# Attention in a two-layer trunk: merge weights applied three heads later through DRAM, output product begun between the last heads' steps

## The chip, the core and the metric

The kernel runs on one core of a Trainium2 chip. The core has five engines with a queue each: TensorE (PE, matmuls and transposes), VectorE (DVE), ScalarE (ACT), GpSimd (POOL) and SyncE (SP); here SP issues every DMA. The metric is device time in microseconds (us) of one launch. The profile is of one execution and names times from the first instruction of its span.

## The reference, cut to what matters

Layer 1 of the trunk mixes tokens by dilated attention: 12 heads in 3 groups of 4 (dilations 1, 4, 16). A group's output is weighted by a softmax over the three groups of a head index, and the 12 weighted outputs go through one output product.

```python
def dilated_attention_mixer(u, w_qkv, w_out, cos, sin):
    ...
    for gi, (window, dilation) in enumerate(DILATED_GROUPS):
        o_g, lse_g = dilated_window_group(q[:, :, hs], k[:, :, hs], v[:, :, hs], window, dilation)
    ...
    alpha = jax.nn.softmax(lse, axis=2)
    o = (o * alpha[..., None]).reshape(B, S, ATTN_WIDTH).astype(u.dtype)
    return o @ w_out
```

All is float32, SEQ = 1024, D_MODEL = 1024, head size 128. After the mixer come the residual, a norm and a dense feed-forward (FFN), then the final norm.

## The kernel before

Activations lie with 128 features on the partitions and 1024 tokens along the row, so a tile is 128x1024 float32. Products are made of pairs: each operand is split into a rounded part and a rest (a cast on ACT, a subtraction on DVE), and three matmuls of 512 columns stand for one (`split`, line 139, `mm3`, line 118, `seeded`, line 706).

The attention pass goes through 12 heads in the order `heads` (line 923): j = 0 to 3 and, within a j, the groups gi = 0, 1, 2. For each head `attn_qk` (line 779) loads two weight tiles, makes seven operands of them (a to g, `pair_weights`, line 691) and runs seven products of 12 matmuls (`pair`, line 727), with rotary embedding (`rope`, line 765) on what comes out. After each product stands a `tick()` (line 720): it runs the steps that `later` put down for this count. So the steps of one head are written between the products of the next: before the change scores at +1 (`s1`) and +3 (`s2`, which ends with the softmax `soft`), the merge weights of a j at +3 after its third head (`attn_weights`, line 892), the transposes of the probabilities at +6 and +8 (`t1`, `t2`), and the product with the values at +10 (`values`, line 874), whose result goes to the DRAM tensor `od`. Seven ticks make one head.

After the last head the remaining ticks run with no product between them (line 938). Then, for all 12 heads, line 943 loads the output from `od`, line 945 loads its merge weight broadcast to all partitions, line 946 multiplies, and line 947 splits the result. `mixer_out` (line 574) then makes eight output tiles in the order `DORDER` (0, 4, 1, 5, ...), each from the 12 splits: 72 matmuls of 512 columns per output tile (12 heads, two halves, three passes).

Tiles come from pools with a fixed number of slots: `ws` 4 (probabilities `ap`, and now the merge tiles), `wx` 2, `vc` 8 (q, k, values, outputs, the two rotary tables), `va` 16 and `vb` 12 (the pass's operands, later the splits), PSUM `mm` 4 and `ax` 4. A request waits for a slot of its tag to come free. The framework's planner fixes the order of each engine's queue from the program's order and its own estimate of when things are ready, so an instruction can stand ahead of its place in the program; the queue is then worked off in that order.

Of the kernel before, what the change touches and what calls it, by code (L numbers as in the profile page):

```python
# [15 lines left out]
P = 128  # L16
T = 1024
# [3 lines left out]
NH = 12  # L21
# [19 lines left out]
def trunk_kernel(ctx, tc, x, cols, consts, w_in, w_hout, w_qkv, w_aout, w_ffn, w_down, out):  # L41
    nc = tc.nc
# [8 lines left out]
    def big(tag, name, dt=F32):  # L51
        return gp.tile([P, T], dt, tag=tag, name=name, bufs=slots[tag])
# [4 lines left out]
    def mmps(name):  # L57
        return pmm.tile([P, 512], F32, tag="mm", name=name)
# [4 lines left out]
    def hs(hh):  # L63
        return slice(hh * 512, hh * 512 + 512)
# [13 lines left out]
    for k in range(KT):  # L78
        t = big("vc", f"x{k}")
# [32 lines left out]
    def load_w(src, n, name, tag="wr"):  # L112
        raw = early.pop(name, None)
        if raw is None:
            raw = load_raw(src, n, name, tag)
        return split_w(raw[:, 0:n], n, name, (256,) if name == "f0" else ())
# [93 lines left out]
    nm = Norm("n0")  # L210
# [7 lines left out]
    for i0 in range(0, NMASK, 8):  # L218
        n = min(8, NMASK - i0)
# [351 lines left out]
        ["vb"] * 2 + ["ws"] * 3 + ["va"] * 16 + ["vb"] * 7,  # L571
    )

    def mixer_out(l, spill, load, vs, parts, name):
        nrm = Norm(name)
        h, ops = {}, {}

        def weights(d):
            n = len(vs) // parts * P
            return [load_w((w_hout, w_aout)[l][d][:, i * n:i * n + n], n, f"{name}w{d}_{i}") for i in range(parts)]  # L580

        for d in DORDER:
            t = big("vc", f"{name}h{d}")
            nc.sync.dma_start(t[:], load[d])
            ws = weights(d)
            if d == KT - 1:
                w_head[l] = ffn_w_head(l, 0)
            ps = [mmps(f"p_{name}{d}_{hh}") for hh in range(2)]
            m = len(vs) // parts
            for i, (whi, wlo) in enumerate(ws):  # L590
                mm3(ps, whi, wlo, 0, vs[i * m:i * m + m], first=(i == 0), last=(i == parts - 1))
            h[d] = add_res(ps, t, d, nrm, spill, 2 * l + 1, name)
            if d >= 4:
                ops[d - 4] = ffn_operands(d - 4, h[d - 4], h[d], op_tags[l][7 * (d - 4):7 * (d - 3)], name)
        return ops, nrm
# [4 lines left out]
    nm = Norm("n2")  # L600
# [116 lines left out]
    def later(n, step):  # L717
        steps.setdefault(n, []).append(step)

    def tick():  # L720
        for step in steps.pop(clock[0], ()):
            step()
        clock[0] += 1
# [55 lines left out]
    def attn_qk(j, gi):  # L779
        n = gi * 4 + j  # L780
        ga = load_raw(w_qkv[n], D, f"aq{n}")
        up = load_raw(w_qkv[NH + n], D, f"ak{n}")
        sz = big("wx", f"sz{n}")
        s5, z = sz[:, 0:512], sz[:, 512:T]
        p = pair(ga, up, qops, s5, f"a{n}")
        q = big("vc", f"aq{n}")
        k = big("vc", f"ak{n}")
        rope(q, next(p), None, 0, z)
        rope(k, next(p), s5, 1, z)
        rope(q, next(p), s5, 1, z)  # L790
        rope(k, next(p), None, 0, z)
        for _ in p:
            pass
        return q, k
# [49 lines left out]
    def attn_value(j, gi):  # L844
        n = gi * 4 + j
        vv = big("vc", f"avv{n}")
        src = vd[:, cs(n)]
        if gi == 0:
            nc.sync.dma_start(vv.rearrange("p (c m) -> p c m", m=P), src.rearrange("(c p) m -> p c m", p=P))
        elif gi == 1:  # L850
            sv = src.rearrange("(i p r) m -> p r i m", p=P, r=4)
            for r in range(4):
                nc.sync.dma_start(vv[:, r * 256:r * 256 + 256].rearrange("p (i m) -> p i m", m=P), sv[:, r])
        else:
            nc.sync.dma_start(vv.rearrange("p (c m) -> p c m", m=P), src.rearrange("(p c) m -> p c m", c=8))
        return vv

    od = dp.tile([NH, P, T], F32, name="od")

    def attn_out(j, gi, blocks, ptiles):  # L860
        dil = (1, 4, 8)[gi]
        n = gi * 4 + j
        pts = {}
        groups = [(t, g1, where[g1:g1 + 4]) for t, where in ptiles for g1 in range(0, len(where), 4)]

        def turn(gs):
            for t, g1, grp in gs:
                ps = axps(f"apx{n}_{grp[0][0]}_{grp[0][1]}")
                for c, key in enumerate(grp):
                    pts[key] = t[:, cs(g1 + c)]  # L870
                    nc.tensor.transpose(ps[:, cs(c)], pts[key], ident)
                nc.scalar.copy(t[:, g1 * P:(g1 + len(grp)) * P], ps[:, 0:len(grp) * P])

        def values(vv):
            o = big("vc", f"ao{n}")
            for hh in range(2):
                ps = axps(f"apo{n}{hh}")
                for b in range(4 * hh, 4 * hh + 4):
                    ks = blocks[b][1]
                    for i, kc in enumerate(ks):  # L880
                        nc.tensor.matmul(ps[:, cs(b % 4)], vv[:, cs(kc)], pts[(b, kc)], start=(i == 0), stop=(i == len(ks) - 1))
                if dil == 1:
                    nc.scalar.copy(o[:, hs(hh)], ps[:])
                else:
                    r = dil // 2
                    sl = slice(hh * r, hh * r + r)
                    nc.scalar.copy(o.rearrange("p (i r) -> p r i", r=dil)[:, sl, :], ps.rearrange("p (r i) -> p r i", r=r))
            nc.sync.dma_start(od[n], o[:])

        return (lambda: turn(groups[:2])), (lambda: turn(groups[2:])), values  # L890

# [29 lines left out]
        return dw  # L921

    heads = [(j, gi) for j in range(4) for gi in range(3)]
    dws = {}
    sts = [sp.tile([P, 3, 8, 2], F32, tag="st", name=f"st{j}", bufs=2) for j in range(4)]
    for i, (j, gi) in enumerate(heads):
        q, k = attn_qk(j, gi)
        blocks, ptiles, s1, s2 = attn_scores(j, gi, sts[j], q, k)
        t1, t2, values = attn_out(j, gi, blocks, ptiles)
        at = clock[0]  # L930
        later(at + 1, s1)
        later(at + 3, s2)
        if gi == 2:
            later(at + 3, lambda j=j: dws.setdefault(j, attn_weights(j, sts[j])))
        later(at + 6, t1)
        later(at + 8, t2)
        later(at + 10, lambda j=j, gi=gi, values=values: values(attn_value(j, gi)))
    while steps:
        tick()
    ov = []  # L940
    for i, (j, gi) in enumerate(heads):
        o = big("vc", f"am{j}_{gi}")
        nc.sync.dma_start(o[:], od[gi * 4 + j])
        wb = big("wx", f"wb{j}_{gi}")
        nc.sync.dma_start(wb[:], dws[j][gi].partition_broadcast(P))
        nc.vector.tensor_mul(o[:], o[:], wb[:])
        ov.append(split(o, "va" if i < 8 else "vb", f"aov{i}"))

    ops, nm = mixer_out(1, hd[2], hd[1], ov, 2, "n3")
    act1 = dp.tile([NF, P, T], F32, name="act1")  # L950
    ffn_in(1, ops, nm, act1)

# [112 lines left out]
```

## Time and profile before

| what | us |
|---|---|
| median of 3 runs | 2611.85 |
| lowest, highest | 2607.98, 2612.05 |
| the profiled execution | 2608.14 |
| its span, first to last instruction | 2606.3 |
| PE busy in the span | 2536.5 |

The attention pass takes about 1412 to 1754 us of the span; from there to about 1825 lie the last heads' steps, the merges, and the first two output tiles. The page gives busy time by engine and the chain of work that ended last; the trace answers for a stretch, an engine, a line or a tile.

### The profile page before, as it was taken

The numbers are of one execution on the slowest core, as the hardware profiler recorded it, in microseconds if no ns is written. First come the engines' busy times: TensorE is split into PE (matmuls) and PEld (weight loads), VectorE is DVE, ScalarE is ACT, GpSimd is POOL, SyncE is SP. The second block draws the span as 40 slices with busy tenths as digits, with TensorE's granted clock in tenths as the row PEclk, the third lists the DMA queues.
The fourth block names the chain that finished last, engine by engine and source line by source line (L and its number), as shares of the span: only waits on it lengthen the run. The fifth ranks groups of instructions, "written<-read, shape, count | busy, mean of one in ns | idle before, by whom it ended". The sixth has DMA issues, their size and how long they took to land.

```text
span 2606.3 us, 30492 instructions
## 1 busy us (share of the span) xinstructions
PE 2536.5 (97%) x11804; PEld 2103.7 (81%) x11804; DVE 1741.4 (67%) x3070; ACT 909.5 (35%) x1400; POOL 129.9 (5%) x107
## 2 busy tenths in 40 slices
PE   8999999999999999999999999998999999999998
PEld 6888888788888888888888777776878888888887
DVE  7888888977877777433613666655477777775336
ACT  5222222344323233212523555653343323332212
POOL 1111111111000000000000000000010000000000
PEclk9999999999999999999999999997999999999999
DMA  4111111142222224531232222227422222236323
GB/s 144 33 33 33 33 33 33 43 144 89 76 87 81 89 81 147 181 104 61 97 105 75 74 66 66 74 90 253 135 81 89 81 89 81 81 102 229 110 58 127
DMA packets 108144, 240.48 MB, mean 92 GB/s; under 512 B 23008, under 2 KB 50016, under 8 KB 108000
## 3 DMA queue, kind: packets, MB, share of 16 engines
q1 hardware_dynamic: 108000, 238.54, 27.9%
q8 instruction: 93, 1.52, 0.2%
q14 instruction: 51, 0.42, 0.1%
HBM read 185.93 MB, written 52.58 MB: 92 GB/s over the span
## 4 chain that ended last, share of the span: by engine, by line
PE 79%; DVE 10%; ACT 4%; DMA 4%; issue 2%; POOL 1%; SPq 0%; POOLq 0%; DVEq 0%; ACTq 0%
PE pt L482 6%; PE pt L483 6%; PE pt L481 6%; PE pfw L125 6%; PE pfw L127 6%; PE pfw L124 6%; PE pb L482 4%; PE pb L483 4%; PE pb L481 4%; PE p_n L125 2%; PE p_n L127 2%; PE p_n L124 2%; PE pv L654 2%; PE pv L655 2%; PE pv L656 2%
## 5 line engine op out<-in xcount | busy, mean ns | idle before, releaser
L563 DVE TENSOR_TENSOR h<-pfw,h 128x512 f32<-128x512 f32 (+1 forms) x104 | 63.6, 645 | 197.6 <-PE pfw L127 197.5
L108 ACT CAST h_fw<-r_fw 128x896 fp32r<-128x896 f32 (+1 forms) x60 | 58.3, 973 | 237.7 <-PE pfw L125 219.5
L108 ACT CAST h_fa<-r_fg 128x1024 fp32r<-128x1024 f32 x44 | 46.5, 1056 | 198.3 <-PE pt L482 183.5
L108 ACT CAST h_fb<-s 128x1024 fp32r<-128x1024 f32 x44 | 46.4, 1054 | 171.1 <-PE pb L482 159.6
L829 PE MATMUL as<-ak,aq 128*128 128x256 f32 (+1 forms) x192 | 65.4, 459 | 20.2 <-DVE ak L777 17.0
L342 DVE COPY_PREDICATED at<-lm,lv 128x192 f32<-128x192 uint8 (+2 forms) x288 | 82.1, 353 | 4.0 <-PE lv L327 3.2
L156 POOL TENSOR_TENSOR rs_n<-ms_n,half 128x8 f32<-128x8 f32 (+2 forms) x7 | 9.3, 1335 | 1357.7 <-DVE ms_n L154 1357.7
L655 PE MATMUL pv<-vw,qb 128*128 128x512 f32 x192 | 74.8, 390 | 0.0
L654 PE MATMUL pv<-vw,qb 128*128 128x512 f32 x192 | 74.8, 389 | 0.0
L656 PE MATMUL pv<-vw,qb 128*128 128x512 f32 x192 | 74.7, 389 | 0.0
L494 DVE TENSOR_TENSOR s<-r_fu 128x512 f32<-128x512 f32 x44 | 30.3, 691 | 64.0 <-DMA r_fu<-in_w_ffn_dram 63.9
L829 PEld LDWEIGHTS as<-ak,aq 128*128 128x128 f32 x192 | 46.0, 279 | 33.6 <-issue 9.2
L482 PE MATMUL pb<-n3b,h_fa 128*128 128x512 f32 x176 | 68.7, 390 | 2.6 <-DVE n3b L456 2.6
L109 DVE TENSOR_TENSOR l_fw<-r_fw,h_fw 128x896 fp32r<-128x896 f32 (+1 forms) x60 | 67.1, 1121 | 4.9 <-ACT h_fw L108 4.3
L482 PE MATMUL pb<-n1b,h_fa 128*128 128x512 f32 x176 | 68.6, 390 | 1.2 <-DVE n1b L456 1.2
L481 PE MATMUL pb<-n3b,h_fa 128*128 128x512 f32 x176 | 68.8, 391 | 0.7 <-ACT n3b L455 0.6
L481 PE MATMUL pb<-n1b,h_fa 128*128 128x512 f32 x176 | 68.6, 390 | 0.0
L481 PE MATMUL pt<-n1t,h_fb 128*128 128x512 f32 x176 | 68.6, 390 | 0.0
L481 PE MATMUL pt<-n3t,h_fb 128*128 128x512 f32 x176 | 68.6, 389 | 0.0
L483 PE MATMUL pb<-n3b,l_fa 128*128 128x512 f32 x176 | 68.5, 389 | 0.0
L483 PE MATMUL pb<-n1b,l_fa 128*128 128x512 f32 x176 | 68.5, 389 | 0.0
L482 PE MATMUL pt<-n3t,h_fb 128*128 128x512 f32 x176 | 68.5, 389 | 0.0
(1504 smaller groups left out, 7939.8 us busy)
## 6 DMA issues: line engine op xcount, KB each, us to landing
r_fu<-in_w_ffn_dram SPq DMA_DIRECT2D x44, 512.0 KB, 3.6
r_fg<-in_w_ffn_dram SPq DMA_DIRECT2D x44, 512.0 KB, 3.6
act<-g SPq DMA_DIRECT2D x44, 512.0 KB, 2.6
st<-act SPq DMA_DIRECT2D x44, 512.0 KB, 4.3
r_fw<-in_w_down_dram SPq DMA_DIRECT2D x44, 448.0 KB, 3.4
h<-hd SPq DMA_DIRECT2D x16, 512.0 KB, 6.3
r_fw<-in_w_down_dram SPq DMA_DIRECT2D x16, 512.0 KB, 3.7
vr<-in_w_qkv_dram SPq DMA_DIRECT2D x24, 256.0 KB, 3.3
```

The lines of the kernel that those rows point to most:

```text
L108: nc.scalar.copy(hi[:, a:b], src[:, a:b])
L124: nc.tensor.matmul(p[:, 0:b - a], wh, vh[:, a:b], start=(first and i == 0), stop=False)
L125: nc.tensor.matmul(p[:, 0:b - a], wh, vl[:, a:b], start=False, stop=False)
L127: nc.tensor.matmul(p[:, 0:b - a], wl, vh[:, a:b], start=False, stop=(last and i == n - 1))
L342: nc.vector.copy_predicated(av[:, :, d:4, :], mk[:, :, d:4, :], pv[:, :, s0:s0 + 4 - d, :])
L481: nc.tensor.matmul(ps[:], wh, bh, start=(kk == 0), stop=False)
L482: nc.tensor.matmul(ps[:], wh, bl, start=False, stop=False)
L483: nc.tensor.matmul(ps[:], wl, bh, start=False, stop=(kk == 3))
L654: nc.tensor.matmul(ps[:], vh, wh, start=(kb == 0), stop=False)
L655: nc.tensor.matmul(ps[:], vh, wl, start=False, stop=False)
L656: nc.tensor.matmul(ps[:], vl, wh, start=False, stop=(kb == 7))
L829: nc.tensor.matmul(ps[:, o:o + w], tok(q, gi, b * P, P), tok(k, gi, ks[0] * P, w), start=True, stop=True)
```

## The change

- The steps of a head move later: scores from +1 and +3 to +2 and +4, transposes from +6 and +8 to +9 and +11, the values product from +10 to +13. The load of the values (`attn_value`) moves from the values step to the first transposes.
- `attn_merge(j - 1)`, after the products of the third head of j: for each of three heads and two halves, load half an output (256 KB) and the broadcast weights (256 KB) into one `ws` tile, multiply on DVE, store back to `od`. Eighteen round trips in all, for j = 0, 1, 2.
- The three outputs of j = 3 stay in SBUF (`late`), and are multiplied there.
- After the loop the nine merged outputs are loaded and split without a multiply. The first two output tiles are begun in between the last steps of the last head: heads 0 to 5 of each, then 6 to 8, and at the end 9 to 11 (`part_out`). `mixer_out` takes them over through `begun`.

```diff
--- before.py
+++ after.py
@@ -571,7 +571,7 @@
         ["vb"] * 2 + ["ws"] * 3 + ["va"] * 16 + ["vb"] * 7,
     )
 
-    def mixer_out(l, spill, load, vs, parts, name):
+    def mixer_out(l, spill, load, vs, parts, name, begun={}):
         nrm = Norm(name)
         h, ops = {}, {}
 
@@ -582,10 +582,10 @@
         for d in DORDER:
             t = big("vc", f"{name}h{d}")
             nc.sync.dma_start(t[:], load[d])
-            ws = weights(d)
+            ws = () if d in begun else weights(d)
             if d == KT - 1:
                 w_head[l] = ffn_w_head(l, 0)
-            ps = [mmps(f"p_{name}{d}_{hh}") for hh in range(2)]
+            ps = begun.get(d) or [mmps(f"p_{name}{d}_{hh}") for hh in range(2)]
             m = len(vs) // parts
             for i, (whi, wlo) in enumerate(ws):
                 mm3(ps, whi, wlo, 0, vs[i * m:i * m + m], first=(i == 0), last=(i == parts - 1))
@@ -857,6 +857,8 @@
 
     od = dp.tile([NH, P, T], F32, name="od")
 
+    late = []
+
     def attn_out(j, gi, blocks, ptiles):
         dil = (1, 4, 8)[gi]
         n = gi * 4 + j
@@ -885,7 +887,10 @@
                     r = dil // 2
                     sl = slice(hh * r, hh * r + r)
                     nc.scalar.copy(o.rearrange("p (i r) -> p r i", r=dil)[:, sl, :], ps.rearrange("p (r i) -> p r i", r=r))
-            nc.sync.dma_start(od[n], o[:])
+            if j < 3:
+                nc.sync.dma_start(od[n], o[:])
+            else:
+                late.append(o)
 
         return (lambda: turn(groups[:2])), (lambda: turn(groups[2:])), values
 
@@ -921,32 +926,67 @@
         return dw
 
     heads = [(j, gi) for j in range(4) for gi in range(3)]
+    def attn_merge(j):
+        for gi in range(3):
+            o = od[gi * 4 + j]
+            for hh in range(2):
+                t = big("ws", f"mg{j}_{gi}_{hh}")
+                oh, wb = t[:, 0:512], t[:, 512:T]
+                nc.sync.dma_start(oh, o[:, hs(hh)])
+                nc.sync.dma_start(wb, dws[j][gi][hs(hh)].partition_broadcast(P))
+                nc.vector.tensor_mul(oh, oh, wb)
+                nc.sync.dma_start(o[:, hs(hh)], oh)
+
     dws = {}
     sts = [sp.tile([P, 3, 8, 2], F32, tag="st", name=f"st{j}", bufs=2) for j in range(4)]
     for i, (j, gi) in enumerate(heads):
         q, k = attn_qk(j, gi)
+        if gi == 2 and j:
+            attn_merge(j - 1)
         blocks, ptiles, s1, s2 = attn_scores(j, gi, sts[j], q, k)
         t1, t2, values = attn_out(j, gi, blocks, ptiles)
+        vv = {}
         at = clock[0]
-        later(at + 1, s1)
-        later(at + 3, s2)
+        later(at + 2, s1)
+        later(at + 4, s2)
         if gi == 2:
-            later(at + 3, lambda j=j: dws.setdefault(j, attn_weights(j, sts[j])))
-        later(at + 6, t1)
-        later(at + 8, t2)
-        later(at + 10, lambda j=j, gi=gi, values=values: values(attn_value(j, gi)))
-    while steps:
-        tick()
-    ov = []
-    for i, (j, gi) in enumerate(heads):
+            later(at + 4, lambda j=j: dws.setdefault(j, attn_weights(j, sts[j])))
+        later(at + 9, lambda t1=t1, vv=vv, j=j, gi=gi: (vv.setdefault(0, attn_value(j, gi)), t1()))
+        later(at + 11, t2)
+        later(at + 13, lambda values=values, vv=vv: values(vv[0]))
+
+
+    ov, begun, aw = [], {}, {}
+    for i, (j, gi) in enumerate(heads[:9]):
         o = big("vc", f"am{j}_{gi}")
         nc.sync.dma_start(o[:], od[gi * 4 + j])
-        wb = big("wx", f"wb{j}_{gi}")
-        nc.sync.dma_start(wb[:], dws[j][gi].partition_broadcast(P))
+        ov.append(split(o, "va" if i < 8 else "vb", f"aov{i}"))
+
+    def part_out(d, lo, hi):
+        if d not in begun:
+            begun[d] = [mmps(f"p_n3{d}_{hh}") for hh in range(2)]
+        i = lo // 6
+        if (d, i) not in aw:
+            aw[d, i] = load_w(w_aout[d][:, i * 768:i * 768 + 768], 768, f"n3w{d}_{i}")
+        mm3(begun[d], *aw[d, i], (lo - 6 * i) * P, ov[lo:hi], first=(lo == 0), last=(hi == NH))
+
+    d0, d1 = DORDER[:2]
+    at = clock[0]
+    for upto, d, lo, hi in ((2, d0, 0, 6), (4, d1, 0, 6), (9, d0, 6, 9), (11, d1, 6, 9), (13, None, 0, 0)):
+        while clock[0] <= at + upto:
+            tick()
+        if d is not None:
+            part_out(d, lo, hi)
+    for gi in range(3):
+        o = late[gi]
+        wb = big("wx", f"wb{gi}")
+        nc.sync.dma_start(wb[:], dws[3][gi].partition_broadcast(P))
         nc.vector.tensor_mul(o[:], o[:], wb[:])
-        ov.append(split(o, "va" if i < 8 else "vb", f"aov{i}"))
-
-    ops, nm = mixer_out(1, hd[2], hd[1], ov, 2, "n3")
+        ov.append(split(o, "vb", f"aov{9 + gi}"))
+    for d in (d0, d1):
+        part_out(d, 9, NH)
+
+    ops, nm = mixer_out(1, hd[2], hd[1], ov, 2, "n3", begun)
     act1 = dp.tile([NF, P, T], F32, name="act1")
     ffn_in(1, ops, nm, act1)
```

## Rows read from the trace of the kernel before

**Rows 1.** The page, parts 1 and 2: engine, busy us; granted clock in 40 slices.

```profile
PE 2536.5 (97%) x11804; PEld 2103.7 (81%) x11804; DVE 1741.4 (67%) x3070; ACT 909.5 (35%) x1400; POOL 129.9 (5%) x107
...
PEclk9999999999999999999999999997999999999999
```

**Rows 2.** Windows: stretch, length, busy us (instructions) by engine, clock, DMA share, GB/s.

```profile
1616.00:1705.00 89.00, 83.94 (x405) 68.95 (x405) 56.38 (x135) 52.20 (x118) 0.00 (x0) 1.00 0.24 71
1735.00:1754.40 19.40, 19.40 (x97) 16.14 (x95) 9.10 (x24) 6.96 (x11) 0.00 (x0) 1.00 0.41 123
1754.40:1761.40 7.00, 3.21 (x14) 1.39 (x13) 3.87 (x7) 6.89 (x22) 0.00 (x0) 0.82 0.07 1
1761.40:1770.00 8.60, 8.22 (x40) 8.02 (x40) 3.38 (x18) 1.75 (x5) 0.00 (x0) 0.75 0.54 170
1770.00:1778.00 8.00, 6.72 (x24) 4.75 (x24) 0.00 (x0) 5.81 (x20) 0.00 (x0) 0.66 0.29 77
1778.00:1783.50 5.50, 0.03 (x1) 0.03 (x1) 1.73 (x5) 2.10 (x3) 0.00 (x0) 0.50 0.74 239
1783.50:1793.00 9.50, 8.58 (x19) 5.80 (x20) 6.51 (x10) 2.13 (x3) 0.00 (x0) 0.50 0.87 289
1793.00:1815.30 22.30, 20.27 (x85) 15.35 (x84) 17.76 (x17) 8.82 (x9) 0.00 (x0) 1.00 0.90 318
1815.30:1825.10 9.80, 9.80 (x43) 7.72 (x42) 6.36 (x7) 3.15 (x4) 0.00 (x0) 1.00 0.85 334
1825.10:1909.00 83.90, 83.90 (x371) 69.32 (x370) 33.97 (x45) 25.17 (x35) 5.16 (x4) 1.00 0.38 124
```

**Rows 3.** Waits of PE over the attention pass, 1412 to 1754: total, times, longest.

```profile
PE as L829 <- DVE ak L777: 14.1, 8, 2.6
PE as L829 <- DVE st L830: 3.1, 3, 1.3
PE p_a L710 <- DVE ak L768: 0.6, 1, 0.6
```

**Rows 4.** Chain that ended last, 1768 to 1783 us: start, us, what.

```profile
1773.58 5.52 DMA dn<-st
...
1780.15 6.01 DMA am<-od
```

**Rows 5.** Timeline of VectorE, a 512-column multiply, the tail's multiply and split.

```profile
1636.88 0.69 DVE L774 TENSOR_TENSOR sz<-sz,sb 128x512 f32<-128x512 f32 x1 [3.51 <-ACT sz L771]
...
1781.11 1.23 DVE L946 TENSOR_TENSOR am<-am,wb 128x1024 f32<-128x1024 f32 x1 [11.62 <-DMA am<-od]
...
1783.45 1.23 DVE L145 TENSOR_TENSOR aov0l<-am,aov0h 128x1024 fp32r<-128x1024 f32 x1 [0.59 <-ACT aov0h L144]
```

**Rows 6.** DMA issues: tensors, count, KB each, us from issue to landing (page; pass).

```profile
vr<-in_w_qkv_dram SPq DMA_DIRECT2D x24, 256.0 KB, 3.3
...
od<-ao SPq DMA_DIRECT2D x12, 512.0 KB, 2.6
...
wb<-dw SPq DMA_DIRECT2D x2, 512.0 KB, 4.6
```

**Rows 7.** Timeline of the SP queue, third cycle of the pass.

```profile
1639.53 0.34 SPq L72 DMA_DIRECT2D r_aq<-in_w_qkv_dram  x1
...
1690.28 0.33 SPq L902 DMA_DIRECT2D cm<-dn  x1
...
1696.24 0.37 SPq L920 DMA_DIRECT2D dw<-ae  x1
```

**Rows 8.** Timeline of ScalarE: a cast that waited for its load, a tail split.

```profile
1676.37 0.62 ACT L611 CAST a7a<-r_aq 128x512 fp32r<-128x512 f32 x1 [3.02 <-DMA r_aq<-in_w_qkv_dram]
...
1782.37 1.04 ACT L144 CAST aov0h<-am 128x1024 fp32r<-128x1024 f32 x1 [3.40 <-DVE am L946]
```

**Rows 9.** Timeline of PE, one scores row and the first product of a head.

```profile
1642.88 2.16 PE L829 MATMUL as<-ak,aq 128*128 128x256 f32 x4 [1.47 <-DVE ak L777]
...
1664.84 0.39 PE L710 MATMUL p_a<-qb,a3a 128*128 128x512 f32 x1
```

## The prediction, made blind

> **What bounds the kernel now.** I read the page first: PE is busy for 2536.5 of 2606.3 us [rows 1], so a gain has to come from stretches in which PE idles or runs slowly. The clock line has one dip, in slice 28, where attention ends and the output product begins. Then the windows, cut at the places where PE's work changes [rows 2]. In a cycle of three heads (1616 to 1705) PE is busy 83.94 of 89.0 us; from 1735 to 1754.4, where the last products run, all of the time. Then it falls: 3.21 of 7.0, 8.22 of 8.6, 6.72 of 8.0, 0.03 of 5.5 us. From 1783.5 to 1793 the granted clock is 0.50, which of the two levels is 1.2 GHz, after PE did almost nothing from 1778 on, and 19 matmuls take 9.5 us. From 1793 the clock is full, but 22.3 us hold 85 matmuls with the DMA engines at 0.90. Only from 1815.3 does the output product run dense.
>
> The waits of PE in the pass itself come next [rows 3]: 14.1 us in 8 waits for the rotated k, the longest 2.6, and 3.1 for the maxima of the scores. Last the chain [rows 4]: the end of the softmax at 1773.58, a 5.52 us store of its sums, then a 6.01 us load of an output just stored. These are round trips through DRAM with nothing beside them.
>
> **The tail, in numbers.** Dense, a matmul of 512 columns costs 83.9 / 371 = 0.226 us [rows 2]. The two first output tiles are 144 of them, 32.6 us. The last heads' transposes, scores and values products are the 3.21 + 8.22 + 6.72 = 18.2 us of PE from 1754.4 to 1778 [rows 2]. Together 50.8 us of work stand in 70.7 us (1754.4 to 1825.1): 19.9 us are lost, and that is the most this end can give.
>
> **What the change makes of the tail.** It removes the serial merge: nine multiplies of 1.23 us on DVE [rows 5], nine broadcast loads [rows 6] and the wait for the last store before the first load; 108 of the 144 matmuls (24.4 us) may run before the last merge weights exist. They go where PE now idles. What still ends last is the chain of the last j. From the end of its softmax: 5.52 us to store the sums [rows 4]; 5.96 us from their load to the store of the weights, as in the cycle before, where no merge stood in DVE's way [rows 7]; that store's landing, for which I take the 2.6 of a store of outputs [rows 6]; 4.6 for the broadcast load [rows 6]; 1.23 to multiply [rows 5] and 1.04 to cast [rows 8]. That is 21 us to the first matmul of head 9. DVE then spends 1.23 + 1.23 us per head on multiply and rest [rows 5], so head 11 is split some 26 us after the softmax and the two tiles are done at 28. If the softmax ended at 1773.6 as now, that is 1801.6, and PE's own sum, 1754.4 + 50.8 = 1805.2, would end last.
>
> It won't end that early, since **slots** are added to the wait. The six merge tiles of j = 2 are requested before the probability tile of the last head, and both come from the four `ws` slots. Two slots come free with the values of head 9, which now run three ticks later, about at the last product (1754); the other two with the values of head 10, well after that. I take it that slots go in order of request. One round of two merge tiles costs a 256 KB load, 3.3 us [rows 6], two multiplies of 512 columns, 1.4 [rows 5], and a store, at most like the 2.6 of one twice its size [rows 6]: 7.3 us, three rounds 22. So the last head's scores have a place at about 1776, the softmax ends near 1785 (now 1773.6), and 28 us later is 1813. Against 1825.1 this gives 12 us; the ends are 19.9 (slots free at once) and 4 (each round loads in the 6.01 us of the load in [rows 4], 2.7 longer, so all is 8 us later). I stay at 12, since the 256 KB row is the nearest in size. A gap of PE before the last three heads is in this forecast; what it may do to the clock is a rival below.
>
> The loads of heads 0 to 8 ask for `vc` slots: the tables, q and k of head 11 and one kept output hold five, so three are open at first, enough for one round of loads and splits in 7 us while the products end. The splits cost 9 x 1.23 us on DVE [rows 5], which had 9.10 + 3.87 + 3.38 + 0 + 1.73 = 18.1 us of work in the 48.5 from 1735 to 1783.5 [rows 2]. They are covered there; without that cover they would cost the 11 us.
>
> **What it makes of the pass.** Scores one tick later put one more product, 12 x 0.226 = 2.7 us, between rope and scores. Every wait for k is at most 2.6 us [rows 3], as the 1.47 before one [rows 9], so the 14.1 us can go in full; at the other end nothing, if the planner puts the scores where it does now. Transposes and values moved later only lengthen lives: q and k are given back one tick later, and the next head's tiles ask a head later. I cost this at nothing, covered by the seven ticks of the next head; without it, the wait for k would come back. I take 11 of the 14.1, as some waits will move to the 3.1 us kind.
>
> The merges of j = 0 and 1 lie inside the pass. DVE gets 12 multiplies of 0.69 us, 8.3 us, in cycles in which it is busy 56.4 of 89 [rows 2]: hidden. SP gets 36 more issues a third of a microsecond each; the queue is idle most of the time, and the next head's weights are ordered at 1639.53 [rows 7] for a product that starts at 1664.84 [rows 9], some 20 us early. What isn't hidden by itself is **waiting in order**: a store waits for its multiply and holds SP's later loads; a multiply waits for two loads and holds DVE's rope and splits, on which PE waits a product later. The trace has no such wait in the pass. Its bounds: a gain is excluded, since nothing is removed there; the low end is nothing, if loads land when the planner expects them; the high end a wait like the 3.02 us of a cast for its load [rows 8] in each of three rounds, 9 us a merge, 18 for two. I take 1.5 us a merge, 3 in all, near the low end, because the weights' loads with 20 us in hand show that DVE's next piece is seldom due at once. So the pass gives 11 - 3 = 8 us.
>
> **Sum.** 12 + 8 = 20 us. The profiled execution, 2608.14 (span 2606.3 and 1.84 around it), becomes 2588; it lay 3.7 us under the median of the runs, so the forecast for the median is 2611.85 - 20 = 2592.
>
> **The rivals.**
> - Slots are no hindrance and the waits vanish whole: 19.9 + 14.1 = 34, 2578. For it: 50.8 us of PE work with no other bound. Against: the order of requests. Chance 0.12.
> - The half clock comes back. PE has 24.4 + 18.2 = 42.6 us to do before the last three heads and is done at 1797, the first matmul of head 9 comes at 1806: 9 us of idling, longer than the 5.5 in which the clock stands at 0.50 now [rows 2]. The last 36 matmuls (8.2 us) and what follows would run at half rate as the 19 do, which took 9.5 us for 4.3 of work: 5 us more, 2597. Chance 0.12. The Trainium skill ("TensorE: Matmul & The Clock Gate", HAM oscillation) says that a gap in which PE idles brings the throttle back and the next group starts cold; the trace agrees, 0.50 from 1778 on.
> - The planner puts the scores where they stood: no 11 us, 12 - 3 = 9, 2603. Chance 0.08.
> - The merges eat the gain: 18 us of waits against 11 + 12, 2607. Within 0.2% of no change. Chance 0.10.
> - **Slower**: DVE stands still behind a multiply or a maximum that waits for a slot, for most of a merge. Three rounds are 22 us; PE can go on for two products, 5.4, before its PSUM tiles are full, so up to 17 us stop per merge, 51 for three, against 25 gained by tail and waits: 2611.85 + 26 = 2638. It decides from 25 / 3 = 8 us a merge on. For it: DVE and SP work in order, and `ws` is shared with the probabilities. Against: the values of the third head before free two slots within a head. Chance 0.13.
>
> The forecast itself has 0.45, its own range 2583 to 2601.
>
> **How the numbers follow.** 0.2% (5.2 us) is about what a measurement of this kernel can tell from no change. Faster: 0.45 + 0.12 + 0.12 + 0.08 = 0.77. Same 0.10, slower 0.13. The range takes in the best case and the one in which the merges eat the gain, and leaves out the slower one: 2577 to 2612.
>
> **What would show it.** In the profile after: fewer and shorter waits of PE for k (14.1 to under 4); matmuls of the output product between 1754 and 1778; clock full there; `dn` stored later than 1773.6; the third output tile begun near 1813 less the 8 of the pass. Wrong would be: VectorE rows that wait for the merge's loads or for its slot for more than a few us, PE rows in the cycle after a merge waiting for DVE, or weights' loads on SP behind a store of `od`.

## The result, and the profile after

| | before | after |
|---|---|---|
| median, us (4 runs each) | 2611.02 | 2633.68 |
| span of the profiled execution | 2606.3 | 2630.1 |
| start of the last matmul of the pass's last product | 1754.17 | 1772.12 |
| start of the first matmul of the third output tile | 1825.11 | 1846.56 |

After over before is 1.0088, 95% interval 1.007 to 1.0105: slower by 22.7 us, where 20 us less were forecast. By the two marks in the table 17.9 us were lost in the attention pass and 3.5 in the tail (from the pass's end to the third output tile: 70.9 us before, 74.4 after).

First the page of after, part 1: busy time by engine.

```profile
PE 2538.7 (97%) x11804; PEld 2110.8 (80%) x11804; DVE 1739.6 (66%) x3079; ACT 908.0 (35%) x1400; POOL 129.9 (5%) x107
```

Over the whole span PE does the same 11804 matmuls in nearly the busy time of [rows 1] (2538.7 against 2536.5 us); what grew is idle time. The windows of after say where (columns as in [rows 2]).

```profile
1437.00:1526.50 89.50, 83.82 (x394) 69.04 (x392) 56.48 (x135) 52.03 (x118) 0.00 (x0) 0.98 0.22 67
1526.50:1616.00 89.50, 78.75 (x365) 65.70 (x366) 52.22 (x122) 42.87 (x94) 0.00 (x0) 0.92 0.35 102
1616.00:1705.00 89.00, 80.15 (x370) 65.06 (x368) 50.55 (x112) 46.07 (x108) 0.00 (x0) 0.96 0.41 114
...
1778.00:1786.00 8.00, 2.95 (x10) 2.47 (x11) 3.57 (x5) 2.98 (x5) 0.00 (x0) 0.59 0.91 291
...
1819.00:1836.00 17.00, 6.77 (x50) 6.10 (x48) 4.04 (x11) 6.39 (x8) 0.00 (x0) 0.84 0.45 126
1836.00:1846.60 10.60, 10.60 (x37) 8.37 (x38) 7.05 (x8) 5.01 (x6) 0.00 (x0) 0.77 0.51 175
```

The first of these cycles holds no merge and is as dense as before. The next two, with the merges of j = 0 and 1, hold 365 and 370 matmuls, where 1616 to 1705 held 405 [rows 2]. Taken head by head (start of one head's first product to the next's), the head that runs during the first merge takes 37.4 us against 29.4 before, and the one during the second 36.2 against 29.8: 8.0 and 6.4 us more. The head ahead of the second merge takes 34.3 against 30.9, but the first load of that merge is issued only at 1677.73, when this head's products end. The other heads differ by up to 2.6 us, both ways.

The waits of PE over the pass of after, 1412 to 1772, then those of VectorE from 1412 to 1860 that name a merge tile (total, times, longest):

```profile
PE as L829 <- DVE st L830: 22.9, 9, 5.6
PE as L829 <- DVE ak L777: 5.2, 5, 1.8
```

```profile
DVE mg L937 <- DMA mg<-dw: 21.8, 9, 4.5
DVE mg L937 <- DMA mg<-od: 9.7, 2, 4.9
```

Against [rows 3], the waits for k shrank from 14.1 to 5.2, and those for the maxima of the scores grew from 3.1 to 22.9. VectorE waited 31.5 us for the loads of the three merges. The timeline of after shows both in the first merge (start, us, engine, line, operation, tiles, idle time before it and what ended that):

```profile
1583.94 0.69 DVE L937 TENSOR_TENSOR mg<-mg 128x512 f32<-128x512 f32 x1 [4.50 <-DMA mg<-dw]
1586.35 0.68 DVE L937 TENSOR_TENSOR mg<-mg 128x512 f32<-128x512 f32 x1
...
1593.16 0.69 DVE L937 TENSOR_TENSOR mg<-mg 128x512 f32<-128x512 f32 x1 [4.92 <-DMA mg<-od]
1594.86 0.69 DVE L937 TENSOR_TENSOR mg<-mg 128x512 f32<-128x512 f32 x1 [1.00 <-DMA mg<-dw]
...
1603.69 0.69 DVE L937 TENSOR_TENSOR mg<-mg 128x512 f32<-128x512 f32 x1 [3.32 <-DMA mg<-dw]
...
1607.31 0.68 DVE L937 TENSOR_TENSOR mg<-mg 128x512 f32<-128x512 f32 x1
1607.91 0.28 DVE L830 CUSTOM_DVE_ANT_0 ap<-as,even 128x128 f32<-128x128 f32 x1
...
1608.26 0.84 PE L829 MATMUL as<-ak,aq 128*128 128x128 f32 x2 [5.58 <-DVE st L830]
```

The six pieces go in three rounds of two, 9.2 and 10.5 us apart, and only behind the sixth does the probability tile of the third head (the one behind whose products the merge is written) get its maxima, on which PE had stood 5.58 us. The SP queue of after in the same rounds:

```profile
1584.66 0.32 SPq L938 DMA_DIRECT2D od<-mg  x1
...
1587.44 0.43 SPq L935 DMA_DIRECT2D mg<-od  x1
...
1594.25 0.88 SPq L72 DMA_DIRECT2D r_aq<-in_w_qkv_dram  x1
```

The next load of a piece is issued 2.8 us after the store of the one before it. The 2.8 is also the landing time of that store, in the rows of DMA issues of after from 1412 to 1772 (tensors, count, KB each, us to landing):

```profile
mg<-od SPq DMA_DIRECT2D x12, 256.0 KB, 5.0
mg<-dw SPq DMA_DIRECT2D x12, 256.0 KB, 5.5
od<-mg SPq DMA_DIRECT2D x12, 256.0 KB, 2.8
```

So a round is a store of 2.8, loads of 5 to 5.5, and a multiply of 0.7: some 9 us, and a little more where one waits its turn. Last the chain of after from the third merge's last multiply on (start, us, what):

```profile
1805.67 0.68 DVE mg L937
...
1818.76 4.85 DMA dn<-st
1823.63 2.46 DMA cm<-dn
...
1829.80 3.79 DMA wb<-dw
...
1835.98 1.65 PE p_n L124 x3
```

The third merge ends at 1806, 34 us after the pass; the sums of the last softmax are stored at 1818.76, and 27.8 us later the third output tile begins. Behind the merge stand the first and the last group of the last head's scores:

```profile
1806.84 1.10 PE L829 MATMUL as<-ak,aq 128*128 128x128 f32 x4
...
1813.17 0.63 PE L829 MATMUL as<-ak,aq 128*128 128x128 f32 x2
```

11 matmuls of the output product stand between these two groups, and one of them waits 1.15 us for its split. So the product that was begun early is itself in the way of the last softmax.

### The profile page after: what moved, and what is told of

It is laid out like the page before. It is cut to its first block, busy times and chain, and to the rows that moved or that the text cites. A ratio compares the mean times of both kernels' runs of the same rounds, so it can differ in the third digit from the quotient of the medians.

```text
span 2630.1 us, 30557 instructions
## 1 busy us (share of the span) xinstructions
PE 2538.7 (97%) x11804; PEld 2110.8 (80%) x11804; DVE 1739.6 (66%) x3079; ACT 908.0 (35%) x1400; POOL 129.9 (5%) x107
## 4 chain that ended last, share of the span: by engine, by line
PE 77%; DVE 9%; DMA 7%; ACT 4%; issue 2%; POOL 1%; SPq 0%; DVEq 0%; POOLq 0%; ACTq 0%
PE pt L483 6%; PE pt L482 6%; PE pt L481 6%; PE pfw L125 6%; PE pfw L127 6%; PE pfw L124 6%; PE pb L482 4%; PE pb L483 4%; PE pb L481 4%; PE p_n L124 2%; PE p_n L125 2%; PE p_n L127 2%; PE pv L654 2%; PE pv L655 2%; PE pv L656 2%
## 5 line engine op out<-in xcount | busy, mean ns | idle before, releaser
L829 PE MATMUL as<-ak,aq 128*128 128x256 f32 (+1 forms) x192 | 64.6, 455 | 30.2 <-DVE st L830 22.9
L483 PE MATMUL pt<-n3t,l_fb 128*128 128x512 f32 x176 | 68.7, 390 | 0.0
```

Of the source, the lines that this page charges most:

```text
L483: nc.tensor.matmul(ps[:], wl, bh, start=False, stop=(kk == 3))
L829: nc.tensor.matmul(ps[:, o:o + w], tok(q, gi, b * P, P), tok(k, gi, ks[0] * P, w), start=True, stop=True)
```

## The experiments

The kernel before ran beside each group of runs; ratios are to it. "Pass" and "tail" are worked out from the two marks of the first table, in the profiled execution.

| kernel | median | ratio, interval | pass ends | tail |
|---|---|---|---|---|
| before | 2611 to 2614 | 1 | 1754.2 | 70.9 |
| after | 2633.68 | 1.0088 [1.0070, 1.0105] | 1772.1 | 74.4 |
| e1_ticks | 2613.02 | 0.9999 [0.9989, 1.0008] | 1756.0 | 71.9 |
| e2_merges | 2631.26 | 1.0066 [1.0051, 1.0081] | 1772.2 | 72.2 |
| e4_scores_first | 2634.73 | 1.0078 [1.0061, 1.0095] | 1777.7 | 74.4 |
| e5_no_multiply | 2632.82 | 1.0078 [1.0059, 1.0096] | 1777.3 | 71.6 |
| e6_own_slot | 2616.52 | 1.0008 [0.9999, 1.0018] | 1763.7 | 65.2 |
| e7_spread | 2608.65 | 0.9978 [0.9968, 0.9988] | 1764.8 | 61.5 |
| e8_no_merge | 2611.89 | 0.9992 [0.9983, 1.0001] | 1756.5 | 66.7 |
| e9_part_only | 2606.69 | 0.9970 [0.9960, 0.9981] | 1755.7 | 64.9 |
| e10_spread_old | 2599.08 | 0.9947 [0.9932, 0.9962] | 1759.7 | 53.9 |
| e11_own_spread_old | 2613.85 | 1.0004 [0.9995, 1.0014] | 1774.4 | 55.3 |
| e12_spread_six | 2604.76 | 0.9968 [0.9955, 0.9981] | 1761.2 | 57.5 |
| e13_part_behind | 2606.47 | 0.9974 [0.9963, 0.9984] | 1755.2 | 65.8 |

### Which part costs: e1 and e2

Three theories stood after the result. A: the block of merges costs what was lost, since its pieces hold `ws` slots that the probabilities need. B: the merges cost it, but because VectorE stands behind multiplies whose loads have not landed. C: the later ticks do it. e1 is the kernel before with the later ticks alone:

```diff
-        later(at + 1, s1)
-        later(at + 3, s2)
+        later(at + 2, s1)
+        later(at + 4, s2)
...
+        later(at + 9, lambda t1=t1, vv=vv, j=j, gi=gi: (vv.setdefault(0, attn_value(j, gi)), t1()))
+        later(at + 11, t2)
+        later(at + 13, lambda values=values, vv=vv: values(vv[0]))
```

> The kernel before with the later ticks alone: scores at +2 and +4, transposes at +9 and +11, values at +13, values loaded at the first transposes. No merge in the pass, no output product in the tail's steps. If the later ticks are harmless (theories A and B, which both blame the merges), 2607 to 2615: in the first cycle of the changed kernel, which holds no merge, PE waited 6.3 us for DVE and ACT against 6.0 before, so the wait for k only turned into one for the scores' maxima. If the later ticks cost by themselves (theory C: scores hold PSUM and probability slots longer), 2620 or more.

No change within 0.1%. The waits of PE over its pass show why no gain came of it:

```profile
PE as L829 <- DVE st L830: 18.2, 10, 3.0
PE as L829 <- DVE ak L777: 3.1, 5, 1.2
```

k is no longer late, as planned; now scores matmuls wait for the maxima of the ones before them, 18.2 us in place of [rows 3]'s 3.1. The wait changed its name and did not shrink (21.3 us in sum, 17.2 before). So waits on the maxima of about this sum come with the ticks alone and cost nothing against before; what the merges add to them shows in the longest, 5.6 us in after against 3.0. With these ticks and no merge the pass ends at 1756.0, so by the marks the merges cost the pass of after 16 us; the head ahead of the second merge takes 34.0 us in e1 too.

e2 is the kernel before with the merges through DRAM alone, at the ticks of before and without the early output product:

```diff
+        if gi == 2 and j:
+            attn_merge(j - 1)
         blocks, ptiles, s1, s2 = attn_scores(j, gi, sts[j], q, k)
```

> The kernel before with the merges through DRAM in the pass alone: old ticks, three last outputs kept in SBUF, the other nine loaded and split without a multiply, no output product between the last steps. Theories A (the next scores' tile waits in line for a slot behind six merge tiles) and B (VectorE stands in its queue behind multiplies whose loads have not landed) both expect the pass longer by 8 to 10 us for each of the merges of j = 0 and 1, and the last head's scores some 25 us late: 2628 to 2645. Theory C expects about 2611.

The merges alone cost 17.3 us: the pass ends 18.0 us later by its mark, and the tail is 1.3 us longer, not shorter. They are the part that costs. The pass as one window, before and e2:

```profile
1412.00:1754.20 342.20, 323.87 (x1532) 265.16 (x1530) 219.92 (x503) 194.77 (x428) 0.00 (x0) 1.00 0.25 74
1412.00:1772.20 360.20, 334.41 (x1535) 272.60 (x1533) 229.14 (x516) 194.71 (x428) 0.00 (x0) 0.96 0.33 95
```

As many matmuls take 10.5 us more of PE's busy time, at a granted clock of 0.96 in place of 1.00, and the idle time grows by 7.5. So more than half of what e2's pass loses is slower matmuls, at a clock that falls to its lower level more often, and not waiting. At the old ticks PE waits only 1.5 us for maxima, so e2 doesn't tell A from B; e4 to e7 are for that.

### What in a merge costs: e4, e5, e6

e4 asks whether slots are given in the order of the program: the call of the merge is moved behind the request of the next scores.

```diff
-        if gi == 2 and j:
-            attn_merge(j - 1)
         blocks, ptiles, s1, s2 = attn_scores(j, gi, sts[j], q, k)
+        if gi == 2 and j:
+            attn_merge(j - 1)
```

> The changed kernel with one call moved: the merge of j - 1 is asked for after the scores of the third head of j have got their tile, so that tile is ahead of the six merge tiles in the line for slots. All loads, multiplies and stores are still there. Theory A: the wait of PE for the scores' maxima after a merge goes, the pass gives back most of its 18 us and the last softmax ends early: 2612 to 2621. Theory B: the multiplies hold VectorE as before, 2628 to 2640.

No faster, and in the range of theory B. The timeline of VectorE in e4 at the first merge:

```profile
1611.27 0.68 DVE L937 TENSOR_TENSOR mg<-mg 128x512 f32<-128x512 f32 x1
1611.87 0.28 DVE L830 CUSTOM_DVE_ANT_0 ap<-as,even 128x128 f32<-128x128 f32 x1
```

The maxima still stand behind the sixth multiply, though the program asks for the probability tile first. I read this as the planner giving a slot to the piece whose load can start; shown is that the order of requests in the program doesn't protect the scores.

e5 leaves the 18 multiplies out, so that nine heads' outputs enter the output product unweighted; loads and stores stay.

```diff
                 nc.sync.dma_start(wb, dws[j][gi][hs(hh)].partition_broadcast(P))
-                nc.vector.tensor_mul(oh, oh, wb)
                 nc.sync.dma_start(o[:, hs(hh)], oh)
```

> The changed kernel without the eighteen multiplies of the merges (so the outputs of nine heads go unweighted into the output product); loads, stores and slots stay, and VectorE has nothing of the merge in its queue. Theory A: the scores still wait for the slots, a round is shorter by some 1 to 2 us of 10: 2626 to 2633. Theory B: VectorE is free, the pass gives back its 18 us: 2610 to 2618.

As slow as after, and 15 us above the range of theory B, with no merge work on VectorE that could wait for a load. Its timeline says what the maxima wait for now:

```profile
1607.38 0.29 DVE L830 CUSTOM_DVE_ANT_0 ap<-as,even 128x128 f32<-128x128 f32 x1 [8.86 <-DMA od<-mg]
...
1607.74 1.32 PE L829 MATMUL as<-ak,aq 128*128 128x128 f32 x4 [9.01 <-DVE st L830]
```

The maxima, which write the probability tile, wait 8.86 us for the store of a merge piece: its slot. PE waits 9.01 behind them. The multiply in front of the maxima in after was the place where the wait showed, not its cause.

e6 leaves the merges as a block but takes their tile from a slot of its own, cut out of the bytes of the masks (three pieces per output, one at a time):

```diff
-                t = big("ws", f"mg{j}_{gi}_{hh}")
+                t = gp.tile([P, 768], F32, tag="mg", name=f"mg{j}_{gi}_{a}", bufs=1)
```

> The changed kernel with the merges in a slot of their own: the bytes of the recurrence masks of layer 0, which nobody reads in layer 1, are handed to one merge tile of 768 columns; an output is merged in three pieces (384, 320, 320 columns) instead of two, one piece at a time. Probability slots are then free of merges; the multiplies still stand in VectorE's queue behind their loads. Theory A (the scores' tile waits for merge tiles to give back a slot): the pass ends near 1757 as with the later ticks alone (1756), the last softmax ends within 20 us of it, total 2598 to 2615. Theory B (waiting multiplies in VectorE's queue): 27 multiplies wait for loads instead of 18, pass end at 1770 or later, total 2628 or more.

Against the kernel before that ran beside it, 2.4 us are lost where after loses 22.7, so some 20 come back. With e5 this says what cost them: merge pieces in the slots of the probabilities. It is 1.5 us above theory A's range, though, and its pass ends at 1763.7, some 8 us later than e1's, where A expected about e1's end: one piece at a time has a price too, which e11 takes up.

### Is it the block: e7

e7 is after with one output's merge per head in place of three behind the third:

```diff
-        if gi == 2 and j:
-            attn_merge(j - 1)
+        if j:
+            attn_merge(j - 1, gi)
```

> The changed kernel with the merges spread: after the products of each head (j, gi) only output gi of j - 1 is merged, one round of two tiles per head instead of three rounds after the third. Same transfers, multiplies and slots in sum. Theory A: a score waits for one round of about 10 us at most, most of which the later ticks and other products cover; pass end 1756 to 1764, total 2602 to 2618. Theory B: the same 18 waits of VectorE for loads, pass end about 1772, 2628 to 2636.

This one edit takes after from 22.7 us above before to 5.5 below. Two pieces at a time leave two of the four slots to the probabilities. The pairs aren't free: the pass ends at 1764.8, 8.8 us later than e1's and just past theory A's 1764; the shorter tail (61.5 us) pays for it.

### Where the gain of the tail is: e8, e9, e13

e8 is after without merges in the pass: the weights are multiplied in after the load of each output, as in the kernel before, but the output product begins early. e9 is the same with the ticks of the kernel before (and the pieces of the product behind ticks +1, +3, +6, +8).

```diff
         nc.sync.dma_start(o[:], od[gi * 4 + j])
+        wb = big("wx", f"wb{j}_{gi}")
+        nc.sync.dma_start(wb[:], dws[j][gi].partition_broadcast(P))
+        nc.vector.tensor_mul(o[:], o[:], wb[:])
```

> The changed kernel without the merges in the pass: the nine outputs of j = 0 to 2 are multiplied after their load in the tail, as before; later ticks and the early start of the output product stay. Theories A and B: pass end 1756, and the tail shows what the early start is worth with no merge tile ahead of the last scores: third output tile 55 to 65 us after the pass instead of 71, total 2602 to 2610. If the early start itself costs (theory C'), 2613 or more.

> The kernel before with the early start of the output product alone: old ticks (parts placed after +1, +3, +6 and +8), last three outputs kept in SBUF, nine outputs multiplied after their load. Theories A and B: pass end 1754 and the tail as in the run with later ticks, 2600 to 2608. Theory C' (the early start is what costs): 2613 or more.

The early start alone gains 0.3% at the old ticks. At the later ones it gains 0.1%, with no change inside the interval: e8 lies between its two expectations, with a tail of 66.7 us where 55 to 65 were expected. Here are the first loads of outputs on SP, in e9 and in e8:

```profile
1750.43 5.34 SPq L947 DMA_DIRECT2D am<-od  x2
...
1760.31 1.05 SPq L949 DMA_DIRECT2D am<-od  x2
```

In e9 they are issued 5.3 us before the pass ends and in e8 3.9 us after it; the first matmul of the output product stands 2.3 and 13.5 us after the pass's end. So it is the later ticks, with the product's pieces moved along, that hold the early start back.

In e9 the tail shrinks by 6 us, less than the 19.9 that were lost, and one reason stands in PE's queue:

```profile
1772.25 0.63 PE L829 MATMUL as<-ak,aq 128*128 128x128 f32 x2
...
1778.60 0.63 PE L829 MATMUL as<-ak,aq 128*128 128x128 f32 x2
```

Between these two pairs of the last head's scores stand 22 matmuls of the output product. The last softmax ends 30.2 us after the pass (1785.93), where it took 19.4 in the kernel before; at the later ticks it is 34.0 in e8 against 17.7 in e1. The early start delays the chain that it was to run beside. That chain behind the last softmax in e9:

```profile
1785.93 8.89 DMA dn<-st
1794.89 5.12 DMA cm<-dn
```

The store of 8 KB of sums lasts 8.89 us and the load of 24 KB 5.12, against 5.52 for the same store in [rows 4]. In the 5.2 us before it SP had issued two broadcast loads of 512 KB and four loads of values; that they are the reason is read from this order, and no run takes them away alone. The Trainium skill ("DMA: Bandwidth & Descriptors", Queues, rings and completion order) says that each DMA engine works off a queue's descriptors in ring order; these durations agree with that.

e13 puts the first two pieces of the product behind both halves of the last head's scores:

```diff
-    for upto, d, lo, hi in ((1, d0, 0, 6), (3, d1, 0, 6), (6, d0, 6, 9),
+    for upto, d, lo, hi in ((3, d0, 0, 6), (3, d1, 0, 6), (6, d0, 6, 9),
```

> e9_part_only with the first two pieces of the output product put behind both halves of the last head's scores instead of before and between them. If the tail is bounded by the chain that follows the last softmax (maxima at 1800 against 1782 in the kernel before, third output tile 20 us later), the scores come some 10 us earlier and the kernel gains up to 5 us on e9_part_only: ratio 0.995 or less. If the sum of PE's work and the slots of the loads bound it, the pieces left behind only fill the gap of the softmax instead: ratio 0.997 as e9_part_only, within 0.1%.

As e9, and it doesn't decide what was asked: the sums are stored at 1786.27 (e9: 1785.93), since PE's queue mixes scores and product matmuls almost as before. As in e4, the place in the program is not the place in the queue.

### Both together: e10, e11, e12

e10 is e7 with the ticks and the pieces' places of e9: merges through DRAM, one output per head.

> The changed kernel with one output's merge per head and with scores, transposes and values at the ticks of the kernel before; output product begun early. Theory A (a slot of ws is held by a merge piece from its load to the end of its store, and six pieces behind one another keep the probabilities out): two pieces per head leave two slots for the probabilities, so the pass costs a few us and the tail, freed of nine broadcast loads and nine multiplies, is 61 to 62 us long as in e7_spread. With the ticks of the kernel before it should then be at or below e9_part_only: ratio 0.995 to 0.997. Rival D (each merge costs the pass what it saves the tail, some 8 us of e7_spread's pass): ratio 0.998 to 1.000, slower than e9_part_only.

It is the fastest kernel, 14.7 us below before and 0.2% below e9: past the good end of theory A's range, with a tail of 53.9 us where 61 to 62 were expected. Its waits in the pass (PE; VectorE for merge tiles, 1412 to 1860), the windows behind the pass, and its chain after the last softmax:

```profile
PE as L829 <- DVE ak L777: 14.8, 8, 2.9
PE as L829 <- DVE st L830: 5.2, 3, 2.4
...
DVE mg L937 <- DMA mg<-dw: 2.2, 4, 0.6
```

```profile
1759.70:1786.40 26.70, 25.65 (x122) 20.86 (x121) 19.84 (x37) 21.43 (x50) 0.00 (x0) 1.00 0.86 257
1786.40:1803.00 16.60, 11.99 (x65) 10.10 (x64) 4.38 (x11) 5.08 (x7) 0.00 (x0) 1.00 0.43 123
1803.00:1813.60 10.60, 10.24 (x37) 7.94 (x38) 6.95 (x8) 3.96 (x6) 0.00 (x0) 0.84 0.47 149
```

```profile
1786.37 4.81 DMA dn<-st
...
1791.32 1.73 DMA cm<-dn
```

VectorE waits 2.2 us for merge tiles in place of 31.5. Of the tail's 53.9 us PE is busy for 47.9 and idle for 6.0; before, it was idle for 13.9 of 70.7 (the windows of [rows 2] from 1754.4 to 1825.1). The sums are stored as late as in e9, but with no broadcast loads in the queue the store takes 4.81 and the load 1.73, and the chain to the third output tile is 27.2 us against e9's 34.7. The merges aren't free: the pass ends 5.5 us later than before.

e11 is e10 with the slot of its own from e6:

> As e10_spread_old, but the merge pieces have a slot of their own (three pieces of 384, 320 and 320 columns, one after the other), so that they never meet the probabilities' slots. Theory A: what e10_spread_old still loses in the pass to shared slots is gone, and the waits of PE for the maxima of the scores fall to the 4.5 us of e9_part_only; 1 to 3 us faster than e10_spread_old. Rival D (what is lost is the traffic and the order in the queues, not the slot): no faster than e10_spread_old, since three pieces make more transfers than two.

14.8 us slower than e10, against theory A as I had put it; rival D had this side. All but 1.4 us of it is a longer pass. The waits of SP between 1526 and 1774, and of VectorE and PE there:

```profile
SPq L937 <- DVE mg L936: 47.4, 20, 4.1
SPq L934 <- DMA od<-mg: 38.1, 22, 4.3
```

```profile
DVE mg L936 <- DMA mg<-dw: 22.7, 11, 4.4
```

```profile
PE apo L882 <- DMA avv<-vd: 7.6, 3, 4.0
```

With one slot each piece's load waits on SP for the store of the one before, 38.1 us in 22 waits, and holds the loads behind it; PE waits for values. I read this as the round trip moved from the probabilities to the queues, where e10 hides it with two pieces side by side, once a head. e11 also cuts an output into three pieces in place of two, and a private pool with two slots wasn't run, so the share of the single slot isn't shown.

e12 leaves the third j to multiplies after the load:

```diff
-        if j:
+        if j in (1, 2):
             attn_merge(j - 1, gi)
```

> As e10_spread_old, but the merge weights of the third j are multiplied in after its outputs are loaded, as in the kernel before; only six outputs go through DRAM for it, none of them in the cycle of the last heads. Theory A with a tail bounded by the chain behind the last softmax: three broadcast loads come back into the tail without being late there, and the last cycle of the pass loses nothing, ratio 0.994 to 0.997. Rival D: between e9_part_only and e10_spread_old, 0.997 to 0.999.

At the edge between the two expectations, and 5.7 us above e10: the last softmax stores its sums at 1791.14, 4.8 us later than in e10. So the outputs of j = 2 are worth merging ahead too.

## Why the prediction was wrong, point by point

**The pass: the step that failed.** I costed the merges of j = 0 and 1 at "1.5 us a merge, 3 in all, near the low end". They cost 16 us together by the marks of after and e1, and 18 by those of e2 and before; the heads during them lose 8.0 and 6.4 us. The slots were in the text: for j = 2 I had worked out three rounds through the four `ws` slots, 22 us. The same six pieces meet the same four slots in every merge, and in the pass I priced waits in order instead, by the slack of the weights' loads [rows 7, 9], which don't use `ws`. The bound of 18 for two merges, at the other end, is about what came, and that is luck: it was made of multiplies that wait for loads, and e5 loses as much without any multiply. Part of the loss, more than half in e2, is slow matmuls, which no term held. The rival on the slower side had this mechanism and the point from which it decides, 8 us a merge; of its two forms e5 shows the second, a maximum that waits for a slot. (The 25 us that it sets against are 12 + 11 = 23 in my own terms, so the point is 7.7.) Its argument against, that two slots come free within a head, is not enough: two free slots at a time are what makes three rounds.

**The size of a round.** Predicted 7.3 us, measured 9.2 and 10.5 in the first merge. The load was taken from the 3.3 us of a weights' load of the same size [rows 6]; two loads per piece, of outputs and of broadcast weights, land in 5.0 and 5.5 us. The store (2.6 taken, 2.8 measured) and the multiply held.

**The ticks.** The 11 of 14.1 us didn't come: e1 is 0.9999 of before. "Some waits will move to the 3.1 us kind" was said and taken as 3; nearly all did. The wait for k covered the wait behind it: a scores tile in PSUM, the memory that matmuls write, is given back only when its maxima are taken. The later ticks were costed at nothing for what comes behind the scores; with the early start they aren't free: e8 against e9, and e7 against e10, are 0.2 and 0.3% apart in favour of the old ticks. These pairs move scores, transposes, values and the product's pieces together, so which of them costs isn't shown.

**Slots in order of request.** Wrong as a rule: e4 asks for the scores' tile first, and its maxima still come last. That the order came out right for after proves nothing for the rule.

**The tail.** 12 us were to be gained here and 3.5 were lost. The end of the softmax was to be 1785; in after it is 1818.76. Of the 33.8 us between, 17.9 are the pass, 12 the longer rounds of the third merge (34 us for 22), and the rest is the way from the merge to the softmax's end, 12.4 us for the 9 I had taken, with matmuls of the early product among the scores. The step that was wrong in itself is the cost of the early start, taken at nothing for the last softmax: without any merge it delays the softmax by 10.8 us (e9 against before) and 16.3 (e8 against e1). So that e10 ends it at 1786.37, near my 1785, is luck; no slots hold it up there, and e9 has 1785.93. The "28 us" from the softmax to the end of the two tiles hold as a sum (27.8 in after, 27.2 in e10) by two errors that cancel: the first matmul of head 9 comes after 17.2 and 16.8 us in place of 21, and the rest takes 10.6 and 10.4 in place of 7. That a begun product is worth much once the merges are out of the way was right: the tail of e10 is 17 us shorter than before, between the 12 I took and the 19.9 I had as the most. The sign that I had named, matmuls of the output product between 1754 and 1778, didn't come: the first of after is at 1785.21, 13.1 us behind its pass, much as in e8 (13.5), which has no merge; in e10, at the old ticks, it is at 1759.95, 0.3 behind.

**The half clock.** It came too, smaller than that rival: in after the clock is 0.59 from 1778 to 1786, when PE is busy 2.95 of 8 us, and 0.77 from 1836, where 37 matmuls take 10.6 us; at the 0.226 of full clock [rows 2] they would take 8.4. What I hadn't looked for is the pass. These are a stretch of after right behind the 5.58 us on which PE stood, and one of the kernel before:

```profile
1608.26:1612.00 3.74, 3.74 (x17) 3.74 (x17) 2.44 (x11) 1.12 (x1) 0.00 (x0) 0.50 0.18 70
...
1772.10:1778.00 5.90, 5.71 (x21) 4.30 (x21) 0.00 (x0) 3.71 (x12) 0.00 (x0) 0.53 0.34 83
```

After this stand PE works at 0.50, the level of 1.2 GHz, and the two cycles with merges have 0.92 and 0.96 in the mean where [rows 2] has 1.00: here PE pays for the stop and then for the matmuls behind it. The second line corrects a reading of mine: in the kernel before it wasn't the idle stretch from 1778 on that brought the clock down, since it was 0.53 already from 1772.1 to 1778, with PE busy for 5.71 of 5.9 us.

**SP's issues** in the pass cost nothing that a row shows. The weights' loads, though, did stand behind a store of `od`, as the list of signs said: `r_aq` is issued at 1594.25, 0.4 us after such a store, and the cast of its weights waits 4.67 us for it. It is still 20 us ahead of the product, which starts at 1614.0, so it isn't what stopped PE.

## What to carry to other kernels

A tile that waits for a round trip through DRAM holds its slot from the issue of its load to the landing of its store (the 8.86 us in e5 are a wait for that landing); before it shares a pool with tiles of the critical path, count the rounds, price one with the loads it will really meet, and charge that at every place where the block stands. Spread such pieces until the pool keeps slots for the others: here the same eighteen round trips cost 17.3 us as three blocks (e2), and as nine pairs they left a kernel 0.2% faster than the one without them (e10 against e9). When work is begun early to fill a gap, look at what its instructions do in the queues, and its loads to the small transfers, on the chain that ends the gap: the last softmax came 10.8 us later for it.

## What the runs showed of the hardware

- Transfers of 256 KB from the same queue took 3.3 us as weights [rows 6] and 5.0 to 5.5 as merge pieces.
- An 8 KB store took 4.81, 5.52 and 8.89 us in three kernels (e10, before, e9), so its size doesn't give its time. The longest, and the 7.81 of e13, came behind two broadcast loads and four loads of values.
- Behind a stand of 5.58 us in after, 17 matmuls ran at a granted clock of 0.50; in e2, at 0.96 in the mean of the pass against 1.00, as many matmuls as before took 10.5 us more.
- Whether e11's 14.8 us all come from the queue of SP isn't settled; its rows show waits there, not that they are the whole.
